# An issue order planned with measured durations, and with the price of changing between dense and small products

## The chip, the core and the metric

The kernel runs on one core of a Trainium2 chip. The metric is the device time of one execution in microseconds (us), from the first to the last instruction with what the launch adds around them. The program is built once; the order in which each engine's instructions stand is fixed then, by Python code in the kernel.

## The reference

One layer of a hybrid backbone over 512 latent tokens and 128 context tokens (together T = 640 columns), width D = 1024:

```python
mod = silu(cond) @ ada_w + ada_b                     # 48 columns of 128: shifts, scales, gates
xn = rmsnorm(x) * (1 + sc1) + sh1
rkv, glu_in, gates = split(xn @ w_in)
y_r = rwkv(shift(rkv), lora(xn), state)              # 8 heads, two directions, a scan over tokens
y_c = silu(layernorm(conv31(glu(glu_in)))) @ w_out_conv
merged = sigmoid(gate_r) * (y_r @ w_out_rwkv) + sigmoid(gate_c) * y_c
x = x + g1 * (merged @ w_o)
x = x + g2 * (relu(xn2 @ mlp_w1) ** 2 @ mlp_w2)      # D_FF = 4096
y = rmsnorm(x) * final_g
```

## The kernel before, in words

All activations lie transposed, 128 channels on the partitions and 640 token columns in two halves of 320. There are three stages.

The **setup** (up to about 60 us) forms the modulation of the first norm, xn, and the first low-rank products. The **planned stage** (about 60 to 748 us) holds everything from the input projection to the merge. The **tail** (`w_o` and the two MLP products, lines 1405 to 1562) is one unbroken run of dense products.

A **dense product** is one matmul of a 128x128 weight by 320 columns in fp32r. Each weight is split into a high and a low part (`wh`, `wl`, ScalarE and then VectorE, in `take`, line 241), so each 128x128 block costs three products (`mm3`, line 283). Twelve or 24 of them fill one PSUM bank (`ps_mm`). In the planned stage the dense jobs stand in one list, `todo` (lines 1321 to 1329): the projections of r, k, v for four head pairs p, four GLU blocks, eight gates, then two blocks of the conv side (`side_products("c")`, which need the finished conv branch), the other eight gates, then the blocks of the RWKV side `"r"` and the last of `"c"`. A job that cannot start yet is passed over. Projections and gates read xn (`xh_t`, `xl_t`); the c and r blocks read `ARGH_t`.

**Small products** are fp32 matmuls for the rest. For each head pair p: `prep` (operands), `gram` (line 765), `inverse` (mostly VectorE), `turn` and `fold`, and then the scan `chain(p)` (line 1016) of 20 steps, each of which waits for the last:

```python
mm(ps, ARGH, S)            # 4 products ps_a<-svu_w,ARGH_t
A.activation(S, ps) x2     # ScalarE empties them
mm(sp, BKt, S)             # 4 products ps_b<-svu_w,BKt_w
V.tensor_tensor(S', sp) x2 # VectorE, beside values(): 4 products and 2 ScalarE copies
```

After `chain(p)` comes `post(p)` (line 1073), the group norm of the scan's output. The conv branch is normalised in two halves by `norm_half` (line 1160). 32 columns of the modulation are formed by `ada_late` (line 621): each loads two halves of a weight column into the one buffer `adl_w` (256 KB each) and multiplies each half by four small products `ps_ad<-adl_w,csb_t`; between the halves stands `yield 2.5` (line 391), which puts the second half 2.5 us later by the planner's clock.

**What sets the order.** Each of these is a Python generator, a lane. The loop at lines 1388 to 1403 keeps an estimated time `now[0]`. At each turn it takes the most urgent lane whose due time has come (`pick`), and if there is none, one dense product (`more`). Each matmul moves the clock on by its estimated length (`mm`, line 192); instructions on VectorE, ScalarE and GpSimd get an estimated end (`Timed`, `cost_v`, `cost_a`, `cost_g`), and a lane's next due time follows from that. A lane may also be put off while `hungry()` holds (line 1372): the estimate then sees too few columns going through TensorE, by a credit that falls at `QUOTA * ENTRY / TICK` columns a microsecond. The order of TensorE, VectorE and ScalarE is issued as the loop made it (`manual_schedule`, line 1388). At run time each engine takes its own list strictly in that order and waits at an instruction whose inputs are not there.

Of the kernel before, what the change touches and what calls it, by code (L numbers as in the profile page):

```python
# [11 lines left out]
F32R = mybir.dt.float32r  # L12
# [3 lines left out]
PSUM = bass.MemoryType.PSUM  # L16

P = 128
# [35 lines left out]
NY1, NY2, NY3, CR, HG = 1, 0, 1, 1, 0  # L54
WARM, AHEAD, LATE, SKEW = 9, 3, 0, 2
NW2, GW, GM, GE = 2, 5, 3, 4
RAWS, SPLITS, SWITCH, EXTRA = ["E", "prod"], ["Gf", "Nb", "Gt"], 1, 0
NWR, NWH = 2, 3

YG, YT, YF = 4, 4, 4  # L60
LEAD, SEM, LOAD = 0.40, 0.2, 4.0
# [4 lines left out]
GAP_LORA, GAP_ADA = 1.5, 3.5  # L66
V_STEP = 20
GLU_AT = 12
TICK, ENTRY, QUOTA, CREDIT, DEBT = 3.413, 3060, 1.55, 200, 6000
CST_ID, CST_MASK, CST_SEL, CST_HSEL, CST_LATE = 0, 128, 256, 258, 260  # L70
NCST = 261

# [4 lines left out]
def hybrid_step(ctx: ExitStack, tc: tile.TileContext, I, O):  # L77
# [9 lines left out]
    now, free, last, ready = [0.0], dict(V=0.0, A=0.0, G=0.0), [0.0], {}  # L87
# [22 lines left out]
    def aps_(kw, *names):  # L110
        return sum(hasattr(kw.get(k), "shape") for k in names)

    def cost_v(name, n, src, kw):
        return 0.07 + 0.06 * aps_(kw, "scalar", "scalar1") + n / 960

    def cost_a(name, n, src, kw):
        return (0.08 if src[0].space == PSUM else 0.16) + 0.093 * aps_(kw, "scale", "bias") + n / 1400

    def cost_g(name, n, src, kw):
        return 1.9 if kw.get("op") == ALU.pow else 0.26 + n / 960  # L120
# [49 lines left out]
    warm = sut([P, 512], "warm")  # L170
# [21 lines left out]
    def mm(out, lhsT, rhs, start=True, stop=True, **kw):  # L192
        PE.matmul(out=out, lhsT=lhsT, rhs=rhs, start=start, stop=stop, **kw)  # L193
        cyc = math.prod(rhs.shape[1:]) * (1 if rhs.dtype == F32R else 2 if "is_transpose" in kw else 4)
        m = math.prod(lhsT.shape[1:])
        overlap = 128 // m if m < 128 else 128 // rhs.shape[0]
        cols = cyc * rhs.shape[0] / 128 * (1 if rhs.dtype == F32R else 0.5)
        gated["cols"] += cols
        gated["burst"] -= cols
        gated["credit"] = min(gated["credit"] + cols, CREDIT)  # L200
        kind = (m, rhs.shape[0], rhs.dtype)
        if kind != gated["kind"]:
            advance(now[0] + SWITCH * gated["drain"] / (2400 if gated["warm"] else 1200))
        gated.update(kind=kind, drain=0 if rhs.dtype == F32R else max(cyc, 256) - max(cyc / overlap, 64))
        advance(now[0] + (max(cyc / overlap, 64) + EXTRA) / (2400 if gated["warm"] else 1200))
        ready[out.name] = ("P", now[0] + SEM / 2)
        last[0] = now[0]

    def split(hi, lo, src):
# [1438 lines left out]
```

## Time and profile before

| | us |
|---|---|
| three runs | 1277.59, 1289.3, 1292.56 |
| their median | 1289.3 |
| the profiled execution | 1274.04 |
| its span, first to last instruction | 1272.3 |

The profiled execution is the shortest of the four times; 1.7 us of it lie outside the span. Times in the rows below count from the span's start. `PE` is TensorE's matmuls, `PEld` its weight loads, `DVE` VectorE, `ACT` ScalarE, `SP` the queue that issues the DMAs; `PEclk` 1.00 is 2.4 GHz and 0.50 is 1.2 GHz. An fp32 product shows as two passes, so four small products are counted as eight instructions (x8). The end of a matmul is modelled, so lengths on TensorE are best read from one start to the next.

### The profile page before, as it was taken

The page shows a single profiled execution, that of the slowest core. Times are in us where ns is not written, and L with a number is a line of the kernel's source. Part 1 is how long each engine was busy: PE and PEld are TensorE (multiplying, and loading weights), DVE is VectorE, ACT ScalarE, POOL GpSimd, SP SyncE. Part 2 cuts the span into 40 slices and gives each one's busy share as a digit, 9 for nine tenths or more (in the row PEclk, how much of TensorE's full clock was granted, in tenths as well). Part 3 has the DMA queues.
Part 4 walks back from the last instruction along what each step waited for, and adds up shares of the span by engine and source line. Part 5 has one row for each costly group of instructions (what it writes and reads, how often), then busy time and mean ns, then how long its engine had stood idle before and what let it go on. Part 6 is the DMA issues. An engine that isn't in the chain of part 4 may idle for free.

```text
span 1272.3 us, 31723 instructions
## 1 busy us (share of the span) xinstructions
PE 1219.7 (96%) x13362; PEld 1069.1 (84%) x13362; DVE 739.8 (58%) x1606; ACT 549.7 (43%) x1390; POOL 28.2 (2%) x21
## 2 busy tenths in 40 slices
PE   8998999999999999999998999999999999999996
PEld 5776786767777777777788899999999999999996
DVE  5536587757777777587444665744433443443354
ACT  5545545644565465546552233544412431342130
POOL 0100000000000000000000000000000000000000
PEclk9999998979999999999999999999999999999998
DMA  9456443222433252233216753022222222222222
GB/s 369 157 174 184 145 120 102 83 64 67 137 97 106 86 173 93 83 118 103 74 46 186 258 195 109 26 67 83 69 81 73 77 75 76 75 75 75 75 75 83
DMA packets 82574, 140.42 MB, mean 110 GB/s; under 512 B 17024, under 2 KB 31616, under 8 KB 82432
## 3 DMA queue, kind: packets, MB, share of 16 engines
q1 hardware_dynamic: 82432, 138.39, 33.7%
q8 instruction: 105, 1.72, 0.6%
q14 instruction: 37, 0.30, 0.1%
HBM read 113.52 MB, written 22.22 MB: 107 GB/s over the span
## 4 chain that ended last, share of the span: by engine, by line
PE 86%; DMA 5%; DVE 4%; issue 2%; ACT 2%; SPq 1%; POOL 0%; POOLq 0%; DVEq 0%; ACTq 0%
PE ps_mm L193 46%; PE ps_b L193 24%; PE ps_a L193 7%; PE ps_t L193 7%; PE ps_ad L193 2%; DMA adl_w<-in_adal 2%; DMA adar_s<-in_adaw 1%; DMA z<-tmp 1%; ACT tmp L106 1%; DVE Gt_w L106 0%; DMA prod_w<-in_w 0%; DVE ARGH_t L106 0%; DVE kk_t L106 0%; DVE wl_t L106 0%; DVE vS_w L106 0%
## 5 line engine op out<-in xcount | busy, mean ns | idle before, releaser
L193 PE MATMUL ps_mm<-xh_t,wh_t 128*128 128x320 f32 x648 | 217.5, 336 | 1.8 <-ACT tmp L106 1.8
L193 PE MATMUL ps_mm<-xh_t,wl_t 128*128 128x320 f32 x648 | 213.9, 330 | 0.0
L193 PE MATMUL ps_mm<-xl_t,wh_t 128*128 128x320 f32 x648 | 213.2, 329 | 0.0
L106 ACT ACTIVATE wh_t<-wr_t 128x512 fp32r<-128x512 f32 x146 | 91.7, 628 | 134.1 <-PE ps_b L193 107.0
L106 DVE TENSOR_TENSOR wl_t<-wr_t,wh_t 128x512 fp32r<-128x512 f32 x146 | 100.2, 687 | 76.0 <-ACT wh_t L106 75.2
L193 PEld LDWEIGHTS ps_mm<-xh_t,wh_t 128*128 128x128 f32 x648 | 123.6, 191 | 21.2 <-issue 11.7
L106 ACT ACTIVATE svu_w<-ps_a 64x128 f32<-64x128 f32 x320 | 86.8, 271 | 125.3 <-PE ps_a L193 119.2
L193 PEld LDWEIGHTS ps_mm<-xl_t,wh_t 128*128 128x128 f32 x648 | 123.4, 190 | 13.7 <-issue 9.0
L193 PEld LDWEIGHTS ps_mm<-xh_t,wl_t 128*128 128x128 f32 x648 | 123.5, 191 | 9.9 <-issue 4.4
L106 DVE SCALAR_TENSOR_TENSOR cacc_w<-upad_w,par_t,cacc_w 128x640 f32<-128x640 f32 x90 | 79.2, 880 | 1.9
L193 PE MATMUL ps_mm<-ARGH_t,wh_t 128*128 128x320 f32 x268 | 72.5, 312 | 0.5 <-DVE rS_w L106 0.5
L106 ACT ACTIVATE tmp<-ps_mm 128x320 f32<-128x320 f32 x80 | 34.8, 435 | 86.8 <-PE ps_mm L193 81.7
L106 DVE TENSOR_TENSOR svu_w<-ps_b,Dc_w 64x128 f32<-64x128 f32 x152 | 43.7, 287 | 48.7 <-PE ps_b L193 45.7
L193 PE MATMUL ps_mm<-ARGH_t,wl_t 128*128 128x320 f32 x204 | 64.1, 314 | 0.4 <-DVE wl_t L106 0.4
L106 ACT ACTIVATE mwh<-wr_t 128x512 fp32r<-128x512 f32 x49 | 31.0, 633 | 72.3 <-PE ps_b L193 69.4
L106 DVE SCALAR_TENSOR_TENSOR ARGH_t<-ps_mm,mod_t,ARGH_t 128x320 f32<-128x320 f32 (+2 forms) x45 | 22.6, 512 | 59.3 <-PE ps_mm L193 59.3
L106 DVE TENSOR_TENSOR tmp<-tmp 128x320 f32<-128x320 f32 x64 | 31.1, 489 | 43.3 <-ACT tmp L106 43.2
L106 DVE TENSOR_TENSOR mwl<-wr_t,mwh 128x512 fp32r<-128x512 f32 x49 | 33.8, 690 | 36.9 <-ACT mwh L106 36.9
L193 PEld LDWEIGHTS ps_mm<-ARGH_t,wh_t 128*128 128x128 f32 x268 | 48.2, 190 | 1.3 <-issue 1.0
L106 ACT ACTIVATE BKt_w<-ps_a 32x512 f32<-32x512 f32 (+3 forms) x80 | 40.0, 502 | 17.9 <-PE ps_a L193 17.0
L193 PE MATMUL ps_mm<-xl,wh_t 128*128 128x320 f32 x140 | 43.9, 314 | 0.0
L193 PE MATMUL ps_b<-ARGH_t,wl_t 128*128 128x320 f32 x140 | 43.6, 312 | 0.0
(374 smaller groups left out, 2981.6 us busy)
## 6 DMA issues: line engine op xcount, KB each, us to landing
wr_t<-in_w SPq DMA_DIRECT2D x221, 256.0 KB, 2.7
adl_w<-in_adal SPq DMA_DIRECT2D x64, 256.0 KB, 2.8
adar_s<-in_adaw SPq DMA_DIRECT2D x16, 512.0 KB, 8.4
ARGH_t<-in_x SPq DMA_DIRECT2D x8, 640.0 KB, 6.0
z<-tmp SPq DMA_DIRECT2D x32, 160.0 KB, 2.7
gate<-tmp SPq DMA_DIRECT2D x32, 160.0 KB, 1.9
tA_t<-z SPq DMA_DIRECT2D x8, 320.0 KB, 3.5
ath_t<-z SPq DMA_DIRECT2D x8, 320.0 KB, 4.4
```

The lines of the kernel that those rows point to most:

```text
L106: return f(*args, **kw)
L193: PE.matmul(out=out, lhsT=lhsT, rhs=rhs, start=start, stop=stop, **kw)
```

## The change

The planner's durations are replaced. A VectorE operation now counts 0.155 us and its elements at 960 a microsecond (480 in a scan, 550 in a transpose), where it counted 0.07, 0.06 for each operand by partition, and the elements at 960. ScalarE counts 0.16 or 0.19 at the start instead of 0.08 or 0.16, and 1180 elements a microsecond instead of 1400. A dense product counts 31 cycles more; a change from small to dense counts 250 cycles (`ENTER`) and one from dense to small 220 (`LEAVE`), beside the drain that was counted before. A product's result counts as there 0.2 us after its end (`SEM`), not 0.1. `QUOTA` falls from 1.55 to 1.25. Nothing is computed in another way, and every engine has as many compute instructions as before; only their order differs. The due times that are written as numbers (`yield 2.5`, `GAP_ADA`, `LOAD`, GpSimd's 1.9) stay.

```diff
-RAWS, SPLITS, SWITCH, EXTRA = ["E", "prod"], ["Gf", "Nb", "Gt"], 1, 0
+RAWS, SPLITS = ["E", "prod"], ["Gf", "Nb", "Gt"]
+EXTRA, ENTER, LEAVE = 31, 250, 220
-TICK, ENTRY, QUOTA, CREDIT, DEBT = 3.413, 3060, 1.55, 200, 6000
+TICK, ENTRY, QUOTA, CREDIT, DEBT = 3.413, 3060, 1.25, 200, 6000
     def cost_v(name, n, src, kw):
-        return 0.07 + 0.06 * aps_(kw, "scalar", "scalar1") + n / 960
+        return 0.155 + n / (480 if name == "tensor_tensor_scan" else 550 if name == "transpose" else 960)
     def cost_a(name, n, src, kw):
-        return (0.08 if src[0].space == PSUM else 0.16) + 0.093 * aps_(kw, "scale", "bias") + n / 1400
+        return (0.16 if src[0].space == PSUM else 0.19) + 0.093 * aps_(kw, "scale", "bias") + n / 1180
         if kind != gated["kind"]:
-            advance(now[0] + SWITCH * gated["drain"] / (2400 if gated["warm"] else 1200))
+            enters = (rhs.dtype == F32R) - (gated["kind"] is not None and gated["kind"][2] == F32R)
+            advance(now[0] + (gated["drain"] + (0, ENTER, LEAVE)[enters]) / (2400 if gated["warm"] else 1200))
-        advance(now[0] + (max(cyc / overlap, 64) + EXTRA) / (2400 if gated["warm"] else 1200))
-        ready[out.name] = ("P", now[0] + SEM / 2)
+        advance(now[0] + (max(cyc / overlap, 64) + (EXTRA if rhs.dtype == F32R else 0)) / (2400 if gated["warm"] else 1200))
+        ready[out.name] = ("P", now[0] + SEM)
```

**First place: TensorE, the scan of the last head pair (p = 3), 13 steps before its end.** `svu_w` is the scan's state S, `ps_mm` a gate, `ps_b<-ARGH_t,Gt_w` a product of `fold`, `ones_t` the sums of `norm_half`. In the kernel before, a half step there looks like this:

```order
L193 MATMUL ps_a_7883<-svu_w,ARGH_t 32x64 x4
L193 MATMUL ps_t<-ARGH_t,svu_w 64x32 x4
L193 MATMUL ps_mm<-xh_t,wh_t 128x320
L193 MATMUL ps_mm<-xl_t,wh_t 128x320
L193 MATMUL ps_mm<-xh_t,wl_t 128x320
L193 MATMUL ps_mm<-xh_t,wh_t 128x320
L193 MATMUL ps_mm<-xl_t,wh_t 128x320
L193 MATMUL ps_mm<-xh_t,wl_t 128x320
L193 MATMUL ps_mm<-xh_t,wh_t 128x320
L193 MATMUL ps_mm<-xl_t,wh_t 128x320
L193 MATMUL ps_b_7884<-svu_w,BKt_w 64x64 x4
```

In the changed kernel the last two gate products on xn stand at the top of this piece, and a whole step follows:

```order
L194 MATMUL ps_mm<-xl_t,wh_t 128x320
L194 MATMUL ps_mm<-xh_t,wl_t 128x320
L194 MATMUL ps_b_8657<-ARGH_t,Gt_w 32x32 x16
L194 MATMUL ps_a_8230<-svu_w,ARGH_t 32x64 x4
L194 MATMUL ps_t<-ARGH_t,svu_w 64x32 x4
L194 MATMUL ps_mm<-BK_w,ones_t 128x320 x2
L194 MATMUL ps_b_8231<-svu_w,BKt_w 64x64 x4
L194 MATMUL ps_a_8230<-cst_t,vS_w 32x64 x2
L194 MATMUL ps_a_8230<-cst_t,vr_w 32x64 x2
L194 MATMUL ps_mm<-BK_w,ones_t 128x320 x2
L194 MATMUL ps_a_8230<-svu_w,ARGH_t 32x64 x4
```

What moved are the dense products: when a scan begins, the dense products still to come before the first c block are 1230, 910, 594 and 310 for p = 0 to 3 in the kernel before, and 1217, 880, 432 and 80 in the changed one; 13 steps before the end of the last scan they are 234 and none.

**Second place: TensorE, between the two halves of one column of `ada_late`.** Of the 32 columns of the kernel before, the one with the fewest rows between its halves has ten:

```order
L193 MATMUL ps_ad<-adl_w,csb_t 32x128 x4
L193 MATMUL ps_mm<-xl_t,wh_t 128x320
L193 MATMUL ps_mm<-xh_t,wl_t 128x320
L193 MATMUL ps_mm<-xh_t,wh_t 128x320
L193 MATMUL ps_t<-cst_t,rh_t 64x128 x10
L193 MATMUL ps_mm<-xl_t,wh_t 128x320
L193 MATMUL ps_mm<-xh_t,wl_t 128x320
L193 MATMUL ps_mm<-xh_t,wh_t 128x320
L193 MATMUL ps_mm<-xl_t,wh_t 128x320
L193 MATMUL ps_mm<-xh_t,wl_t 128x320
L193 MATMUL ps_mm<-xh_t,wh_t 128x320
L193 MATMUL ps_ad<-adl_w,csb_t 32x128 x4
```

In the changed kernel the first column reads:

```order
L194 MATMUL ps_ad<-adl_w,csb_t 32x128 x4
L194 MATMUL ps_mm<-xh_t,wh_t 128x320
L194 MATMUL ps_mm<-xl_t,wh_t 128x320
L194 MATMUL ps_mm<-xh_t,wl_t 128x320
L194 MATMUL ps_mm<-ARGH_t 128x320
L194 MATMUL ps_t<-ARGH_t 128x320
L194 MATMUL ps_mm<-xh_t,wh_t 128x320
L194 MATMUL ps_mm<-xl_t,wh_t 128x320
L194 MATMUL ps_mm<-xh_t,wl_t 128x320
L194 MATMUL ps_ad<-adl_w,csb_t 32x128 x4
```

The same first column has 19 rows between its halves in the kernel before; over all 32 columns the middle number falls from 18 to 14. Over the whole of TensorE's order the changes between dense and small products fall from 762 to 678.

## Rows read from the trace of the kernel before

**Rows 1.** Windows by stage: length, busy us (instructions) by engine, PEclk, DMA share, GB/s

```profile
60.00:640.00 580.00, 552.67 (x8727) 427.74 (x8727) 401.62 (x903) 313.18 (x907) 15.67 (x8) 0.98 0.36 112
640.00:681.00 41.00, 38.57 (x375) 32.96 (x374) 18.63 (x51) 19.08 (x50) 3.16 (x2) 1.00 0.24 79
681.00:745.00 64.00, 58.59 (x386) 56.32 (x385) 39.27 (x77) 16.94 (x32) 0.00 (x0) 1.00 0.78 254
745.00:1272.30 527.30, 514.38 (x3504) 513.36 (x3503) 244.74 (x495) 169.05 (x330) 3.40 (x4) 0.99 0.24 76
```

**Rows 2.** Timeline of PE, start us and length: a group of small products between dense ones

```profile
243.36 0.41 PE L193 MATMUL ps_mm<-xl_t,wh_t 128*128 128x320 f32 x1
243.61 0.31 PE L193 MATMUL ps_mm<-xh_t,wl_t 128*128 128x320 f32 x1
243.75 0.31 PE L193 MATMUL ps_mm<-xh_t,wh_t 128*128 128x320 f32 x1
243.90 0.30 PE L193 MATMUL ps_mm<-xl_t,wh_t 128*128 128x320 f32 x1
244.04 0.31 PE L193 MATMUL ps_mm<-xh_t,wl_t 128*128 128x320 f32 x1
244.28 0.32 PE L193 MATMUL ps_a<-svu_w,ARGH_t 128*32 128x64 f32 x8
```

**Rows 3.** Waits of PE from 60 to 745 us: total us, times, longest

```profile
PE ps_ad L193 <- DMA adl_w<-in_adal: 8.8, 7, 2.7
PE ps_t L193 <- DVE kk_t L106: 6.5, 5, 3.1
PE ps_t L193 <- DVE vS_w L106: 5.3, 5, 1.6
```

**Rows 4.** The tile adl_w, and its products in the timeline of PE (60 and 570 us)

```profile
DMA to landing us min/median/max: 2.5/2.8/5.2
60.82 0.43 PE L193 MATMUL ps_ad<-adl_w,csb_t 128*32 128x128 f32 x8
66.41 0.43 PE L193 MATMUL ps_ad<-adl_w,csb_t 128*32 128x128 f32 x8
...
570.46 0.42 PE L193 MATMUL ps_ad<-adl_w,csb_t 128*32 128x128 f32 x8
573.65 0.43 PE L193 MATMUL ps_ad<-adl_w,csb_t 128*32 128x128 f32 x8
```

**Rows 5.** Timeline of all engines: a step of the last scan, and a dense product behind

```profile
640.20 0.32 PE L193 MATMUL ps_a<-svu_w,ARGH_t 128*32 128x64 f32 x8
640.65 0.57 ACT L106 ACTIVATE svu_w<-ps_a 64x128 f32<-64x128 f32 x2 [0.30 <-PE ps_a L193]
640.81 0.56 PE L193 MATMUL ps_mm<-xh_t,Gf_w 128*128 128x320 f32 x2
641.59 0.45 PE L193 MATMUL ps_b<-svu_w,BKt_w 128*64 128x64 f32 x8
642.09 0.61 DVE L106 TENSOR_TENSOR svu_w<-ps_b,Dc_w 64x128 f32<-64x128 f32 x2 [0.28 <-PE ps_b L193]
642.22 0.41 PE L193 MATMUL ps_mm<-xh_t,Gf_w 128*128 128x320 f32 x1
642.36 0.57 ACT L106 ACTIVATE svu_w<-ps_a 64x128 f32<-64x128 f32 x2 [0.33 <-PE ps_a L193]
```

**Rows 6.** Timeline of PE: the last scan's first and last step, post, first c block

```profile
579.15 0.32 PE L193 MATMUL ps_a<-svu_w,ARGH_t 128*32 128x64 f32 x8
656.46 0.32 PE L193 MATMUL ps_a<-svu_w,ARGH_t 128*32 128x64 f32 x8
668.02 1.09 PE L193 MATMUL ps_t<-cst_t,rh_t 128*64 128x128 f32 x16
670.33 0.41 PE L193 MATMUL ps_mm<-xh_t,wl_t 128*128 128x320 f32 x1
680.64 0.56 PE L193 MATMUL ps_mm<-ARGH_t,Nb_w 128*128 128x320 f32 x2 [1.09 <-ACT Nb_w L106]
```

**Rows 7.** The stretch at half clock and the one behind it (windows), and PE in the first

```profile
272.00:289.00 17.00, 16.80 (x180) 12.60 (x180) 7.39 (x20) 5.98 (x19) 0.00 (x0) 0.50 0.15 47
289.00:306.00 17.00, 17.00 (x226) 12.34 (x222) 13.87 (x45) 8.23 (x19) 0.00 (x0) 1.00 0.20 63
279.08 0.44 PE L193 MATMUL ps_a<-svu_w,ARGH_t 128*32 128x64 f32 x8
281.91 0.70 PE L193 MATMUL ps_b<-svu_w,BKt_w 128*64 128x64 f32 x8
282.53 0.32 PE L193 MATMUL ps_a<-cst_t,vS_w 64*32 64x64 f32 x2
```

## Prediction

> **What bounds the kernel now.** I read the windows by stage first. In the planned stage (60 to 640 us) PE is busy 552.7 of 580 us, in the tail 514.4 of 527.3, and no other engine comes near [rows 1]. So time goes down only if PE needs less for its products, or waits less. The room is small: the idle time of PE between 60 and 640 us is 27.3 us, and between 640 and 681 us 2.4 us [rows 1]. The list of PE's waits says what ends that idle time: 8.8 us are the loads of `adl_w`, and 6.5 and 5.3 us are VectorE's emptying of the one bank `ps_t` inside a group norm, which stands in one piece of code and cannot be filled by any order [rows 3].
>
> "Perfetto Trace Analysis" of the Trainium skill, section "Identifying the Most-Contended Engine", says that matmul busy time is a bad measure of the distance from the limit and that the share of weight loads is a good one. By it PE has 580 - 427.7 = 152 us of room in the planned stage [rows 1], and a better order could win far more than I allow. I follow the idle time instead: small products hold PE while their weight loads are short, and in the tail, where nothing but dense products stands, both readings come to the same (514.4 and 513.4).
>
> The second thing to read is where the dense products stand, because they are what fills PE while a scan step waits. In the trace the last scan begins at 579.15 and its last step stands at 656.46; the post work ends at 670.33, and the first c block starts at 680.64 [rows 6]. In the order of before, dense products lie in every half step up to that point. In the changed order the scan of p = 3 starts with 80 of them left instead of 310, and for its last 13 steps, for `post(3)` and up to the first c block there are none. The c blocks cannot come forward: they need the conv branch.
>
> **The change part by part.**
>
> First, fewer changes between dense and small. From one dense product to the next it is 0.14 to 0.15 us (243.61 to 243.75); from the first one behind a small group 0.25 (243.36 to 243.61), from the last one in front of a group 0.24 (244.04 to 244.28) [rows 2]. A visit to the small products thus costs 0.10 + 0.09 = 0.19 us. Over the whole order there are 762 - 678 = 84 changes fewer; in the planned stage alone 88, which is 44 visits: 44 x 0.19 = 8.4 us less. The last product of a group also runs longer, but groups of unlike small products now follow each other 32 times more; these two take most of each other back, and I leave them out. Bounds: 0 to -12.
>
> Second, the loads of `adl_w`. There is one buffer, so the second half's load starts when the first half's products are done, and lands 2.5 to 5.2 us after its issue, 2.8 in the middle. The shortest distance between two halves is 570.46 to 573.65, 3.2 us; the first one took 60.82 to 66.41, 5.6 us [rows 4]. Half a column is 0.36 us of products, so about 3.0 us of other work are needed between them, more in the first 120 us where the weights' loads share the queue. The due time of 2.5 us is unchanged, but the planner's clock was slow: it charged a dense product 320/2400 = 0.133 us, where a row shows 0.146, and nothing for the 0.19 of a visit. With the new numbers 2.5 planned us are close to 2.5 real ones. Counting the products between the halves in the changed order with the lengths of rows 2 and 5, 17 of 32 columns have less than 3.0 us between them, where before it was two. Ten of these miss by about 0.5 us; seven early ones by some 1.5. That is 15 us, against the 8.8 of before, which go: +7. What waits behind it on PE is everything, since PE takes its list in order. Bounds: 0 (loads land at their minimum) to +20 (all 17 as late as the first one, 2 us and more).
>
> Third, the bare end of the last scan. What was hidden there is now in the open. One step is: four products to the end of ScalarE's two copies, 640.20 to 641.22, 1.02 us; then four products to the end of the copies behind `values`, 641.59 to 642.93, 1.34 us [rows 5]. With 0.1 us for each of the two releases of PE (an estimate; ScalarE starts 0.13 us behind the products in rows 5) a step cannot take less than 2.4 to 2.6 us. PE itself works only 0.61 + 0.63 = 1.24 us in it (640.20 to 640.81, 641.59 to 642.22). An idle PE has lost its clock in this trace: at 1.2 GHz the same groups take 0.44, 0.70 and 0.32 us instead of 0.32, 0.45 and 0.25 [rows 5, 7], some 0.4 us a step. So a step takes about 2.9 us: 13 x 2.9 = 38. The conv branch's normalisation runs on the same ScalarE and VectorE in this time; I add 3 us for that. From the last step to the first c block it took 24.2 us (656.46 to 680.64 [rows 6]), of which 111 gate products (counted in the order) of 0.147 us are 16 us. Without them 8 us of PE's work remain, but the group norm is a chain through ScalarE, VectorE and GpSimd, and the c weights must be split: between 8 and 24 I take 16, the middle. Together 38 + 3 + 16 = 57 us. PE's own work in it is 13 x 1.24 = 16 for the steps and about 12 for the rest (two sums of `norm_half` and `post`, the first group of which is the 1.09 us of rows 6), 28 us, which the kernel before did too. About 3 us of waits stood in this stretch before and are replaced (the 2.4 us of idle time in 640 to 681 [rows 1]). Loss: 57 - 28 - 3 = +26. Bounds: 13 steps of 2.4 and 8 us behind them, 39 us, +8; 13 steps of 4.1 us, which is what a step took with its dense products (77.3 us from the first to the last, 19 steps [rows 6]), and 24 behind them, 77 us, +46.
>
> On the clock, "TensorE: Matmul & The Clock Gate" of the Trainium skill, section "Terms", puts the price of a throttled time at that time x (1 - K/N). If the whole bare stretch of 57 us went at 1.2 GHz, this would be 28 us on top. The rows give less: at half clock 180 instructions went through in 17 us, in the next 17 us 226 [rows 7], a fifth fewer and not half, since small products wait on their neighbours more than on the array. I keep the rows' 0.4 us a step, 5 us in all.
>
> Nothing is expected behind that point: the c and r blocks stand in the same number and nearly the same sequence (first c block to the end of the span 591.7 us [rows 1, 6]), and the tail is the same list.
>
> Sum: -8 + 7 + 26 = +25. The profiled execution took 1274.0 us (span 1272.3), so 1299 on its basis. It is the fastest of four; the middle of 1274.0, 1277.6, 1289.3 and 1292.6 is 1283.4, and the median of the three runs 1289.3. A measured median should stand as far above the fastest as it did before: I add 9.4 us for that and forecast 1308. Each change below is likewise set on 1283.4.
>
> **Rivals.**
>
> The waits of before go, and the bare stretch is cheap (not slower). The estimate now has the measured lengths, so a lane should be taken when its operands are really there. For it: 27.3 us of idle PE in the planned stage, of which 27.3 - 6.5 - 5.3 = 15.5 can be moved by an order, and two stretches where the clock fell. Against it: the longest of these waits hangs on a due time that did not change, and three quarters of the last scan's dense cover (310 to 80) is gone in the order itself. With all 15.5 gone, -8 for the changes and the bare stretch at its lower bound of +8, the sum is -15, about 1268; with the bare stretch at +20 it is -3, 1280. It decides when the bare stretch costs less than the 24 us that the other two give.
>
> The bare stretch is dearer (much slower). ScalarE has in it four scan copies of 0.28 us and up to two more small ones a step, and 17 operations for each half of the conv norm; every engine takes its list in order, so a norm copy that waits for GpSimd holds up a scan copy behind it. Steps of 3.7 us, between my 2.9 and the 4.1 of before, and 24 us behind them give 72 - 28 - 3 = +41; with -8 and +15 for the loads this is +48, 1331.
>
> The order change comes to nothing (same): the earlier dense work is not lost, and the scan was not late. For it: all 310 products are done in any case. Against it: they lie ahead of the scan and not beside it. Here PE would reach the last scan 15 us sooner than the count of its products says; +0 to +8, 1283 to 1291.
>
> **How the numbers follow.** A measurement of this kernel can tell about 1% (13 us) from no change. Forecast, +13 to +38: 0.60. Waits gone: 0.12, half of it beyond -1%. Dearer: 0.16. Nothing: 0.12. Faster by over 1%: 0.06. Within 1%: 0.06 + 0.12 = 0.18. Slower: 0.60 + 0.16 = 0.76. The range leaves out half of the first rival and the upper end of the second: 1281 to 1335.
>
> **What would show it.** Right: between about 645 and 700 us PE is busy for half the time or less with nothing dense in it; its clock falls there; the waits of PE on `svu_w` rise from almost nothing to 10 us or more; the first c block starts at 700 to 712 instead of 680.6, and from there to the end it is 590 to 595 us as before. The waits for `adl_w` rise from 8.8 to about 15. From a dense product to the next it stays 0.146. Wrong: the first c block starts before 690, which would mean that steps of the scan are shorter than 2.4 us or that PE came to the last scan earlier than its count of products says; or the loss lies in the c and r blocks, behind that point.

## The result: slower by 3.8%, twice the loss that was forecast

| | before | after |
|---|---|---|
| median of four runs, us | 1286.2 (1277.6 to 1292.6) | 1337.1 (1326.4 to 1337.8) |
| ratio of after to before, 95% interval | | 1.038 (1.030 to 1.047) |
| profiled execution, us | 1274.0 | 1326.4 |
| its span, us | 1272.3 | 1324.6 |

The forecast was +25 us (1308, range 1281 to 1335); measured are +51. The direction and the main term were right, the size was not, and the time lies 2 us outside the range. Both profiled executions lie 11 to 12 us below the medians, and as far apart (52 us) as these are (51).

**The windows by stage** of the changed kernel, against [rows 1], with the same columns (length, then busy us and instructions of PE, PEld, DVE, ACT, POOL, then PEclk, DMA share, GB/s). The first three stretches have the same limits as in [rows 1]:

```profile
60.00:640.00 580.00, 536.42 (x8151) 423.63 (x8150) 379.42 (x844) 288.55 (x813) 15.31 (x7) 0.96 0.36 113
640.00:681.00 41.00, 40.72 (x625) 31.97 (x623) 21.79 (x48) 21.81 (x80) 0.85 (x1) 0.91 0.09 28
681.00:745.00 64.00, 47.15 (x424) 38.53 (x424) 27.11 (x73) 24.70 (x70) 3.22 (x2) 0.58 0.24 72
745.00:1324.60 579.60, 560.64 (x3799) 557.89 (x3797) 277.75 (x560) 183.07 (x358) 3.40 (x4) 0.99 0.28 92
```

PE's idle time up to 640 us is 43.6 us where it was 27.3, and between 681 and 745 us 16.9 where it was 5.4, with a granted clock of 0.58.

**The waits of PE** from 60 to 745 us, against [rows 3]:

```profile
PE ps_ad L194 <- DMA adl_w<-in_adal: 21.8, 19, 3.2
PE ps_t L194 <- ACT Gf_w L107: 6.3, 1, 6.3
PE ps_mm L194 <- DVE wl_t L107: 5.0, 1, 5.0
PE ps_a L194 <- ACT svu_w L107: 4.8, 7, 0.7
PE ps_t L194 <- DVE vS_w L107: 4.6, 5, 1.4
PE ps_t L194 <- DVE kk_t L107: 3.9, 6, 0.9
```

The loads of `adl_w` cost 21.8 us where they cost 8.8. The next two, one wait each, are as good as new (`wl_t` cost 0.4 us before, `Gf_w` nothing), and neither was in the forecast.

**The last scan in PE's timeline**, against [rows 5, 6]: its first step, the last gate product on xn, the first step behind it, its last step, `post(3)`, the first c block:

```profile
635.71 0.32 PE L194 MATMUL ps_a<-svu_w,ARGH_t 128*32 128x64 f32 x8
...
663.11 0.31 PE L194 MATMUL ps_mm<-xh_t,wl_t 128*128 128x320 f32 x1
...
663.73 0.32 PE L194 MATMUL ps_a<-svu_w,ARGH_t 128*32 128x64 f32 x8
...
707.84 0.44 PE L194 MATMUL ps_a<-svu_w,ARGH_t 128*32 128x64 f32 x8 [0.69 <-ACT svu_w L107]
719.91 1.97 PE L194 MATMUL ps_t<-cst_t,rh_t 128*64 128x128 f32 x16 [2.54 <-POOL rh_t L107]
723.44 0.90 PE L194 MATMUL ps_mm<-ARGH_t,wh_t 128*128 128x320 f32 x2
```

From the last gate product to the first c block it is 60.3 us: 44.1 us of bare steps (a bare step has no dense product in it; 663.73 to 707.84) and 15.6 us behind them. One step and the start of the next (timeline of PE, ScalarE, VectorE) show what a step waits for: PE waits for ScalarE's copies, and operations of the conv norm stand between these in ScalarE's list. In the first step one of them (`pt_t<-BK_w`) fits into a gap and holds nothing up. In the second, `BK_w` runs until 699.47 and the scan's copy starts at 699.49, though its products started at 698.47; the first step takes 2.9 us, the second 3.4.

```profile
694.94 0.57 ACT L107 ACTIVATE svu_w<-ps_a 64x128 f32<-64x128 f32 x2 [0.27 <-PE ps_a L194]
695.41 0.55 ACT L107 ACTIVATE pt_t<-BK_w,hlnb_t 128x320 f32<-128x320 f32 x1
695.56 0.44 PE L194 MATMUL ps_a<-svu_w,ARGH_t 128*32 128x64 f32 x8 [0.69 <-ACT svu_w L107]
696.12 0.57 ACT L107 ACTIVATE svu_w<-ps_a 64x128 f32<-64x128 f32 x2 [0.17 <-PE ps_a L194]
696.45 0.98 PE L194 MATMUL ps_b<-svu_w,BKt_w 128*64 128x64 f32 x8
697.47 0.61 DVE L107 TENSOR_TENSOR svu_w<-ps_b,Dc_w 64x128 f32<-64x128 f32 x2 [0.16 <-PE ps_b L194]
697.87 0.55 ACT L107 ACTIVATE svu_w<-ps_a 64x128 f32<-64x128 f32 x2 [0.72 <-PE ps_a L194]
698.47 0.44 PE L194 MATMUL ps_a<-svu_w,ARGH_t 128*32 128x64 f32 x8 [0.67 <-ACT svu_w L107]
698.91 0.56 ACT L107 ACTIVATE BK_w<-BK_w,par_t 128x320 f32<-128x320 f32 x1
699.49 0.57 ACT L107 ACTIVATE svu_w<-ps_a 64x128 f32<-64x128 f32 x2
```

**Where the 52 us are.** Both kernels issue the same products, so the two lists can be laid side by side by position. For each kind of neighbours on PE (dense to dense, dense to small, and so on) I took the mean distance from start to start in the trace of before, without the places where PE stood idle, and added these up along each list: this is the list's own work. What a trace takes above it is waiting and slow clock.

| part of PE's list | before | after | difference |
|---|---|---|---|
| own work up to the first c block | 630 | 620 | -10 |
| above it, up to the last gate product of after (about the 5400th product) | 48 | 71 | +23 |
| above it, from there to the first c block | 2 | 32 | +30 |
| above it, in the two c blocks (96 products; 16.7 us before, 26.4 after) | 3 | 12 | +10 |
| above it, behind them | 8 | 7 | -1 |

The sum is +52, the difference of the spans. The split depends on how the neighbours are sorted: by shape, by tile or only as dense and small, with or without the idle places, the first row comes out between -8 and -16, the second between +18 and +25, the third between +30 and +35, and the c blocks at +10.

### The profile page after: what moved, and what is told of

It is laid out like the page before. It is cut to its first block, busy times and chain, and to the rows that moved or that the text cites. A ratio compares the mean times of both kernels' runs of the same rounds, so it can differ in the third digit from the quotient of the medians.

```text
span 1324.6 us, 31765 instructions
## 1 busy us (share of the span) xinstructions
PE 1240.0 (94%) x13362; PEld 1090.7 (82%) x13362; DVE 741.3 (56%) x1606; ACT 549.1 (41%) x1390; POOL 28.8 (2%) x21
## 4 chain that ended last, share of the span: by engine, by line
PE 82%; DMA 6%; DVE 6%; ACT 3%; issue 2%; POOL 0%; SPq 0%; POOLq 0%; DVEq 0%; ACTq 0%
PE ps_mm L194 43%; PE ps_b L194 24%; PE ps_t L194 7%; PE ps_a L194 7%; DMA adl_w<-in_adal 4%; PE ps_ad L194 2%; DMA pg_t<-g 1%; ACT svu_w L107 1%; DVE vS_w L107 1%; DVE prod_w L107 1%; DVE Gt_w L107 1%; DVE cacc_w L107 1%; DVE ARGH_t L107 0%; DMA ARGH_t<-in_x 0%; DVE wl_t L107 0%
## 5 line engine op out<-in xcount | busy, mean ns | idle before, releaser
L194 PE MATMUL ps_mm<-xh_t,wh_t 128*128 128x320 f32 x680 | 226.3, 333 | 0.4 <-ACT tmp L107 0.3
L194 PE MATMUL ps_mm<-xh_t,wl_t 128*128 128x320 f32 x680 | 225.3, 331 | 0.0
L194 PE MATMUL ps_mm<-xl_t,wh_t 128*128 128x320 f32 x680 | 225.2, 331 | 0.0
L194 PEld LDWEIGHTS ps_mm<-xl_t,wh_t 128*128 128x128 f32 x680 | 131.4, 193 | 13.9 <-issue 8.6
L194 PEld LDWEIGHTS ps_mm<-xh_t,wl_t 128*128 128x128 f32 x680 | 131.1, 193 | 14.0 <-issue 9.8
L194 PEld LDWEIGHTS ps_mm<-xh_t,wh_t 128*128 128x128 f32 x680 | 131.2, 193 | 13.2 <-issue 6.4
L107 ACT ACTIVATE svu_w<-ps_a 64x128 f32<-64x128 f32 x320 | 86.8, 271 | 122.5 <-PE ps_a L194 117.8
L194 PE MATMUL ps_mm<-ARGH_t,wh_t 128*128 128x320 f32 x284 | 77.5, 318 | 1.1 <-ACT wh_t L107 0.6
L194 PEld LDWEIGHTS ps_mm<-ARGH_t,wh_t 128*128 128x128 f32 x284 | 52.3, 196 | 2.0 <-ACT wh_t L107 0.9
L194 PE MATMUL ps_ad<-adl_w,csb_t 128*32 128x128 f32 x512 | 28.4, 295 | 22.0 <-DMA adl_w<-in_adal 21.8
L194 PEld LDWEIGHTS ps_mm<-ARGH_t,wl_t 128*128 128x128 f32 x212 | 40.8, 192 | 5.4 <-DVE wl_t L107 5.4
```

The costliest lines, as they stand in the source:

```text
L107: return f(*args, **kw)
```

## The experiments

A time from one run is held against the profiled execution of the changed kernel, 1326.4. The four runs of that kernel span 11 us, so a difference of less than that says nothing by its time; there the parts of the trace have to speak.

**1. The old lengths of VectorE and ScalarE, everything else new.**

```diff
     def cost_v(name, n, src, kw):
-        return 0.155 + n / (480 if name == "tensor_tensor_scan" else 550 if name == "transpose" else 960)
+        return 0.07 + 0.06 * aps_(kw, "scalar", "scalar1") + n / 960
     def cost_a(name, n, src, kw):
-        return (0.16 if src[0].space == PSUM else 0.19) + 0.093 * aps_(kw, "scale", "bias") + n / 1180
+        return (0.08 if src[0].space == PSUM else 0.16) + 0.093 * aps_(kw, "scale", "bias") + n / 1400
```

> The changed kernel with the old lengths for VectorE and ScalarE; the new ones for TensorE, SEM and QUOTA 1.25 stay. In its order no step of the last scan is bare (570 dense products left when it starts, instead of 80) and there are 692 changes instead of 678. My theory (the bare end of the scan cost about 30 us, the c blocks right behind it 10, the loads of adl_w 13, and the lengths of VectorE and ScalarE are what made the scan late): the bare end and the loss in the c blocks go, the waits on adl_w are about 12 to 16 us instead of 21.8, and the time is 1275 to 1295, level with the kernel before. Rival (the loss is spread over the whole planned stage by the new lengths for TensorE and the lower QUOTA): it stays above 1310.

Measured: 1284.0 us (ratio to before 0.998, 0.994 to 1.001). The profiled execution took 1291.1 us and has 15.9 us of waits on `adl_w`. Its windows from 640 us on, in the columns above:

```profile
640.00:681.00 41.00, 39.28 (x269) 38.37 (x266) 18.43 (x31) 18.79 (x38) 0.00 (x0) 0.99 0.48 153
681.00:745.00 64.00, 62.12 (x415) 60.54 (x414) 28.93 (x55) 16.59 (x32) 0.00 (x0) 1.00 0.62 190
```

1.9 us of idle PE stand between 681 and 745 us instead of 16.9, at full clock: the bare end and the loss in the c blocks went together. The rival falls. Which of the two engines' lengths does it in the changed kernel, this run does not tell; experiment 10 takes ScalarE's alone, on the kernel before. That longer lengths push a lane's small products back, and so let dense ones go first, follows from the planner's code and from the counts in the orders; no run shows it step by step.

**2. QUOTA alone.**

```diff
-TICK, ENTRY, QUOTA, CREDIT, DEBT = 3.413, 3060, 1.55, 200, 6000
+TICK, ENTRY, QUOTA, CREDIT, DEBT = 3.413, 3060, 1.25, 200, 6000
```

> The kernel before with QUOTA 1.25 instead of 1.55 and nothing else. Its order has 648 changes instead of 762 (57 visits fewer) and no bare step; when the last scan starts, 506 dense products are left instead of 310. My theory (a visit costs 0.19 us, and QUOTA is not what made the scan late): 57 x 0.19 = 11 us less on TensorE, a few us of it given back in waits on adl_w (nine columns with little between their halves instead of six), so 0.5% faster, 1273 to 1288. Rival (QUOTA alone does the damage): 1310 or more.

Measured: 1293.3 us (ratio 1.006, 1.002 to 1.011). Neither theory. PE's waits from 640 to 745 us show why:

```profile
PE ps_mm L193 <- ACT wh_t L106: 13.3, 2, 12.7
PE ps_t L193 <- ACT pt_t L106: 3.6, 1, 3.6
PE ps_t L193 <- ACT u_t L106: 1.7, 1, 1.7
```

The scan has its cover, but the norm of the conv branch stands last in this order, with 7 dense products behind its sums (216 before). They run out at 670 us, and PE has next to nothing until the first c block at 696.5: about 26 us. I had looked for bare steps of the scan only. Up to the last gate product the kernel was indeed ahead; the end took it all back.

**3. No load for the second half of a modulation column** (the weights of the first half are multiplied again, so half of each column is left out).

```diff
-            raw = wt([P, KD // 2, P], "adl")
-            DMA.dma_start(out=raw, in_=I["adal"][col - 16, :, 4 * j:4 * j + 4, :])
+            if j == 0:
+                raw = wt([P, KD // 2, P], "adl")
+                DMA.dma_start(out=raw, in_=I["adal"][col - 16, :, 0:4, :])
```

> The changed kernel without the second half's load of adl_w: the second half of each of the 32 columns multiplies the weights of the first half again (the second half of each column is left out of the computation). TensorE's order stays. My theory: the waits on adl_w fall from 21.8 us to 5 or less, TensorE reaches the last gate product 15 to 20 us earlier, and the bare end stays at about 60 us; 1310 to 1322 in all. Rival (another wait takes the place of the load, since lanes that were covered by it come up next): the time falls by less than 8 us.

Measured (one run): 1308.2 us, 18 less. The waits on `adl_w` fell to 2.0 us, the last gate product came at 645 instead of 663, and the stretch behind it took 60.8 us, as in the changed kernel (60.3). Nearly all that the loads cost is real; the wait of 6.3 us on `Gf_w` stayed (6.5).

**4 and 5. Dense products that nobody needs in the bare end: clock or latency?** The first kernel asked for the bank anew for each product:

```diff
+        if steps[3] and 3 not in chained and not any(j[1] is gate for j in todo):
+            mm(bank("ad")[:, 0:H2], xh[:, 0, 0:P], xh[:, 0, 0:H2])
+            return True
```

> The changed kernel with 172 dense products more, which multiply xn by itself into a bank that nobody reads, in the bare end of the last scan and only there; nothing is left out. They let TensorE's list there look as in the kernel before. Theory (the bare end is a chain of latencies; the clock of 1.2 GHz that was granted there is a smaller part): the granted clock goes up to 2.4 GHz, the stretch from the last gate product to the first c block stays at 52 to 60 us, and the c blocks behind it, which began at 1.2 GHz, take 2 to 4 us less. Rival (the clock sets the pace of the bare steps): with the clock at 2.4 GHz the stretch falls to 45 us or less although TensorE has 25 us more work in it.

Measured (one run): 1443.9 us. It answers nothing: there is one buffer for this bank (`ps_ad`), so each added product's weight load waited 0.41 us for the product before, and they stood 0.69 us from start to start where dense ones stand 0.15. The second kernel keeps the bank and allows six products a step (the expectation calls the first ones fp32; the trace has them in one pass each, as dense ones):

```diff
+        if steps[3] and 3 not in chained and not any(j[1] is gate for j in todo) and fillt.count(steps[3]) < 6:
+            if not fillt:
+                fillt.append(bank("ad"))
+            mm(fillt[0][:, 0:H2], xh[:, 0, 0:P], xh[:, 0, 0:H2])
+            fillt.append(steps[3])
+            return True
```

> The changed kernel with 82 dense products more (xn by itself, into a bank that nobody reads), at most six in a step of the last scan where nothing else is left; the first such kernel was made with 172 fp32 products of 0.62 us at 1.2 GHz, so it told nothing of the clock. These add 12 us of TensorE's work at 2.4 GHz to a stretch in which it was busy for about 40 of 60 us. Theory (a chain of latencies): whether or not the clock rises, the stretch from the last gate product to the first c block stays between 52 and 64 us. Rival (the clock sets the pace): if the clock is 2.4 GHz there, the steps take 2.6 us or less and the stretch 50 us or less in spite of the added work.

Measured (one run): 1338.9 us; the stretch took 65.2 us, 1 more than my theory's upper end. Windows of it (columns as above), and the starts of three steps in PE's timeline:

```profile
707.00:724.00 17.00, 14.59 (x191) 11.28 (x183) 8.82 (x30) 10.25 (x30) 0.00 (x0) 0.85 0.12 32
724.00:735.00 11.00, 8.46 (x97) 6.08 (x92) 4.55 (x16) 4.47 (x14) 0.00 (x0) 1.00 0.04 13
```

```profile
718.71 0.32 PE L194 MATMUL ps_a<-svu_w,ARGH_t 128*32 128x64 f32 x8
...
722.30 0.32 PE L194 MATMUL ps_a<-svu_w,ARGH_t 128*32 128x64 f32 x8
...
725.07 0.32 PE L194 MATMUL ps_a<-svu_w,ARGH_t 128*32 128x64 f32 x8
```

Its last five steps ran at 2.4 GHz (0.32 us for a group that takes 0.44 at 1.2) and still took 2.8 to 3.6 us, against 2.9 to 3.4 at half clock in the changed kernel. The rival wanted 2.6 us or less. But the clock rose for only a part of the stretch, and the six added products of a step take about 0.9 us (estimate: six times 0.147), so the run bounds the clock's part and doesn't measure it. Experiment 7 does.

**6. A longer due time between the halves, on top of experiment 1.**

```diff
-            yield 2.5 if k0 == 0 else 0.0
+            yield 3.6 if k0 == 0 else 0.0
```

> The changed kernel with the old lengths for VectorE and ScalarE, and with the due time between the two halves of a modulation column at 3.6 instead of 2.5 us. In its order one of 32 columns has too little between its halves (ten without the longer due time), no step of the last scan is bare, 565 dense products are left when it starts, and there are 658 changes. My theory (15.9 us of waits on adl_w stood in the kernel without the longer due time, and what waits is the load's own 2.8 us): they fall to 5 us or less, and the time is 8 to 14 us less than that kernel's 1284, about 1270 to 1276, 1% faster than the kernel before. Rival (the modulation columns come later and something else runs out): 1280 to 1295.

Measured: 1270.3 us (ratio 0.989, 0.985 to 0.993), 1.1% faster than the kernel before, at the lower end of what I expected. The first of PE's waits from 60 to 745 us, and the windows behind 640 us:

```profile
PE ps_ad L194 <- DMA adl_w<-in_adal: 6.5, 4, 3.1
```

```profile
640.00:681.00 41.00, 41.00 (x281) 41.00 (x280) 11.95 (x18) 13.08 (x25) 0.00 (x0) 1.00 0.50 159
681.00:745.00 64.00, 61.36 (x409) 59.61 (x408) 35.83 (x71) 15.79 (x31) 0.00 (x0) 1.00 0.70 229
```

The loads cost 6.5 us instead of 15.9, and PE is idle for 2.6 us from 640 to 745 us, all of it at full clock.

**7. The same due time on the changed kernel alone.** The edit is that of experiment 6.

> The changed kernel with 3.6 us between the halves of a modulation column and nothing else. In its order two columns are short instead of 23, but three dense products are left when the last scan starts, and 19 of its steps are bare instead of 13. My theory (both are terms of one sum): the waits on adl_w fall from 21.8 to 6 us or less, -16; six bare steps more at 3.0 us less 1.24 of their own work, +10; 1325 to 1335, about level with the changed kernel. Rival (the waits on adl_w were the larger part): 1315 or less.

Measured (one run): 1308.8 us. The rival's number. The waits on `adl_w` fell to 1.7 us and the one on `Gf_w` to 0.5, and at the last gate product PE stood 42 us above its own work instead of 71: 29 us, not 16, of which these two waits are 26. The bare end grew more than I thought: 86.8 us, of which 40.8 are own work, so 46 instead of 32, or 2.3 us for each of six more steps where I had 1.8.

This run also measures the clock's part of a bare step. One step ran at 2.4 GHz, the last of several at 1.2 GHz, with the same 32 instructions on PE and nothing added (PE's timeline, from one step's start to the next):

```profile
645.08 0.32 PE L194 MATMUL ps_a<-svu_w,ARGH_t 128*32 128x64 f32 x8
...
647.77 0.32 PE L194 MATMUL ps_a<-svu_w,ARGH_t 128*32 128x64 f32 x8 [0.69 <-ACT svu_w L107]
...
685.44 0.44 PE L194 MATMUL ps_a<-svu_w,ARGH_t 128*32 128x64 f32 x8 [0.69 <-ACT svu_w L107]
...
688.50 0.44 PE L194 MATMUL ps_a<-svu_w,ARGH_t 128*32 128x64 f32 x8 [0.69 <-ACT svu_w L107]
```

It took 2.7 us; the seven such steps at half clock took 2.9 to 3.4, 3.2 in the mean (3.1 in the changed kernel). Experiment 10 has one more bare step at 2.4 GHz, without any hold on ScalarE, of 2.4 us (672.61 to 675.05), where the shortest ones at half clock took 2.9. So the clock is worth about 0.5 us of a bare step, and most of the step's length stays without it. These are two steps, and the norm's operations fall differently in each, so the figure is good to some 0.2 us.

**8. QUOTA 1.25 with the conv lane more urgent** (to mend experiment 2).

```diff
-URGENT = dict(scan=0, split=0.3, shift=1.45, post=1, side=0.9, solve=1, prep=1.5, lora=2, ada=4, out=4.5, branch=0.5, conv=1.6)
+URGENT = dict(scan=0, split=0.3, shift=1.45, post=1, side=0.9, solve=1, prep=1.5, lora=2, ada=4, out=4.5, branch=0.5, conv=1.2)
```

> The kernel before with QUOTA 1.25 and with the conv lane's urgency at 1.2 instead of 1.6, and nothing else. With QUOTA 1.25 alone the norm of the conv branch came last: 7 dense products were left behind its sums, TensorE then stood 26 us nearly idle, and the whole was 0.6% slower than before. Here 285 are left behind these sums and 425 when the last scan starts; the changes fall to 568. My theory (visits cost 0.19 us, and what was lost with QUOTA alone was only that the dense products ran out ahead of the norm): the 26 us go, some 5 us more of adl_w waits come (18 columns short instead of nine), and the time is 1268 to 1278, 1% faster than before. Rival (fewer changes mean a lower clock or longer waits elsewhere, which was what made QUOTA 1.25 slow): 1284 or more.

Measured: 1332.1 us (ratio 1.039, 1.033 to 1.046). A clear miss. The bare 26 us did go, and its list has the least own work of all these kernels that keep a cover (609 us to the first c block, 21 less than before). But PE stood 131 us above that work at the first c block, against 50. Its window up to 640 us and PE's two longest waits from 60 to 745 us:

```profile
60.00:640.00 580.00, 520.80 (x8143) 410.47 (x8142) 377.65 (x845) 284.29 (x812) 15.06 (x7) 0.88 0.34 104
```

```profile
PE ps_ad L193 <- DMA adl_w<-in_adal: 21.4, 13, 4.9
PE ps_a L193 <- ACT svu_w L106: 9.3, 15, 0.7
```

With 568 changes the dense products stand in longer runs and the small ones in longer runs between them. There the steps wait for their copies, the loads for their landing, and the clock falls (0.88). How much of the loss comes from the longer runs, and how much from the conv lane's new place, these two runs don't separate: experiment 2 has 648 changes and lost 0.6%. The theory that fewer changes are worth their visits falls, as a forecast of the whole; the price of a visit is not touched.

**9. Only the due time of post(3)'s last product.**

```diff
-        yield 3.0
+        yield 3.0 if p < 3 else 6.0
         V.tensor_tensor(out=y, in0=y, in1=g, op=ALU.mult)
```

> The changed kernel with one due time changed: in post(3) the product with g stands 6.0 planned us behind the load of g instead of 3.0, so that VectorE's splits of the c weights stand ahead of it in VectorE's list. My theory (VectorE waited 3 us for the load of g, and the splits and TensorE's c products behind it): the wait of 5.0 us in the c blocks goes, and they take 20 to 23 us instead of 26.4. Rival (the splits are late for another reason, their load or ScalarE's copy): a wait of 4 us or more stays at the same product.

Measured (one run): 1324.5 us, too near to tell from 1326.4, and the c blocks take 25.3 us instead of 26.4. In the changed kernel VectorE's list had the product with g ahead of the splits, and PE's c block waited behind both (timeline of VectorE and PE):

```profile
727.88 0.83 DVE L107 TENSOR_TENSOR vS_w<-vS_w,pg_t 128x640 f32<-128x640 f32 x1 [3.05 <-DMA pg_t<-g]
728.62 1.29 DVE L107 TENSOR_TENSOR wl_t<-wr_t,wh_t 128x512 fp32r<-128x512 f32 x2
...
729.36 0.64 PE L194 MATMUL ps_mm<-ARGH_t,wl_t 128*128 128x320 f32 x1 [5.02 <-DVE wl_t L107]
```

With the edit that wait is 1.1 us, and the next one takes most of its place, 6.6 instead of 3.9: ScalarE's `Nb_w` stands behind its copies of post(3)'s output, which is now stored later. PE's timeline with the edit:

```profile
721.96 0.64 PE L194 MATMUL ps_mm<-ARGH_t,wl_t 128*128 128x320 f32 x1 [1.14 <-DVE wl_t L107]
745.19 6.92 PE L194 MATMUL ps_mm<-ARGH_t,Nb_w 128*128 128x320 f32 x24 [6.57 <-ACT Nb_w L107]
```

The mechanism (a wait at the head of an engine's list) is right, the price of mending one place is not: the whole chain behind the last scan is late.

**10. The new lengths of ScalarE alone, on the kernel before.**

```diff
     def cost_a(name, n, src, kw):
-        return (0.08 if src[0].space == PSUM else 0.16) + 0.093 * aps_(kw, "scale", "bias") + n / 1400
+        return (0.16 if src[0].space == PSUM else 0.19) + 0.093 * aps_(kw, "scale", "bias") + n / 1180
```

> The kernel before with the two new constants of ScalarE's lengths and nothing else. Its order has none of the dense products left when the last scan starts (310 before), so all 20 steps of it are bare, and 678 changes. My theory (the cover of the last scan decides, whatever the new length was that took it away): 20 steps of 3 us and 16 us behind them stand where TensorE has 20 x 1.24 + 12 = 37 us of its own work, +39; the c blocks behind them cost 10 more as in the changed kernel: 1286 + 49, between 1315 and 1345. Rival (it takes the new lengths of all engines together): 1280 to 1300.

Measured: 1337.1 us (ratio 1.040, 1.035 to 1.044). The time is as expected; two constants of an engine that is busy for half the time are as bad as the whole change. The parts are not as expected. From the last gate product (601.6) to the first c block (732.6) it is 131 us, where the theory had 76 for the steps and what follows them. The 39 us before the scan's first step (640.8) are bare as well, and PE is busy for half of them (window, columns as above):

```profile
600.00:641.00 41.00, 21.34 (x646) 18.44 (x644) 32.66 (x74) 11.99 (x29) 1.96 (x1) 0.57 0.19 61
```

Ahead of that PE loses less than in the kernel before: when both have done 565 us of their own work, 26 us stand above it instead of 45, and this makes up for it. So the time was met by luck in part; that a lost cover is dear stands. The c blocks behind the bare end take 27.3 us.

**11. The new lengths of TensorE alone, QUOTA left at 1.55.**

```diff
-RAWS, SPLITS, SWITCH, EXTRA = ["E", "prod"], ["Gf", "Nb", "Gt"], 1, 0
+RAWS, SPLITS = ["E", "prod"], ["Gf", "Nb", "Gt"]
+EXTRA, ENTER, LEAVE = 31, 250, 220
...
-        ready[out.name] = ("P", now[0] + SEM / 2)
+        ready[out.name] = ("P", now[0] + SEM)
```

> The kernel before with the new lengths for TensorE alone (EXTRA, ENTER, LEAVE, SEM) and QUOTA left at 1.55. The order puts nearly all dense products first: 864, 168, 0 and 0 are left at the four scans, 40 steps are bare, 112 changes stand where there were 762. My theory (a charge for dense products and QUOTA are one setting: at 1.55 the planner is always short of columns): the 325 visits fewer give 60 us, and 40 bare steps with 3.0 - 1.24 each cost 70, with the bare prep and post between them 50 to 90 more; 1340 to 1400. Rival (the changes were the cost): 1230 or less.

Measured (one run): 1430.5 us, worse than my range. The list's own work fell by some 60 us as counted, and some 250 us of waits and slow clock stand above it at the first c block. The charges of TensorE and QUOTA are one setting: with the same charges and QUOTA 1.25 (experiment 1) the time is 1284.0.

**12. Experiment 6 with QUOTA 1.4.**

```diff
-TICK, ENTRY, QUOTA, CREDIT, DEBT = 3.413, 3060, 1.25, 200, 6000
+TICK, ENTRY, QUOTA, CREDIT, DEBT = 3.413, 3060, 1.4, 200, 6000
```

> The changed kernel with the old lengths for VectorE and ScalarE, 3.6 us between the halves of a modulation column, and QUOTA 1.4 instead of 1.25 (the best kernel so far has 1.25). 448 dense products are left at the last scan instead of 565, two columns are short instead of one, 678 changes instead of 658. My theory (QUOTA sets how evenly the dense products are spread, and with them the granted clock; the kernel with 1.25 spent 51 us of its first 1000 at 1.2 GHz, the kernel before 31): some 20 us less at 1.2 GHz, each worth 0.2, is 4 us, less 2 us for 10 visits more: 1264 to 1272. Rival (the cover is thinner and the time is the same or worse): 1272 or more.

Measured: 1269.2 us (ratio 0.987, 0.983 to 0.991). The time is within the range, and the interval overlaps that of experiment 6, so the two are not told apart. The reason doesn't hold: its profile has 61 us at 1.2 GHz in the first 1000, more and not less than the 51 of experiment 6; its waits on `adl_w` are 0.8 us. This and experiment 6 are the versions that beat both kernels, the one before by little over 1%.

## Why the prediction was right in direction and half in size

**First term, fewer changes, -8.** The list's own work is 10 us less. Right as a term. Experiment 8 shows that it can't be sold alone: what shortens the list takes the cover from the waits.

**Second term, the loads, +7: the step that failed most.** It counted 17 columns with less than 3.0 us of other work between their halves and let ten miss by 0.5 us and seven by 1.5, some 15 us. In the trace 17 columns do wait between their halves, and 15 of them have 1.2 to 3.0 us of other work there (two have 3.2 and 3.3), so the count was good. The need of 3.0 us was too small: in these 17 columns it is 2.65 to 5.2 us from the end of the first half to the start of the second, 3.7 in the middle, since the load has to be issued first and then lands in 2.5 to 4.7 us. Their waits are 1.13 us in the mean, 19.2 us. Two more waits, 2.6 us, stand ahead of a column's first half, where the term did not look. Together that is 21.8 us, +13 where +7 stood. The trace of before could have said that the line is not sharp: four of its seven waits are in columns with 3.5 to 4.1 us of other work, 0.4 to 2.2 us each.

And the term had nothing else in it: the part of the list up to the last gate product lost 23 us. The other 10 are the wait on `Gf_w`, 6.3, and an estimated 3 to 4 of slow clock (up to that product 44 us at 1.2 GHz instead of 27; the 17 us more at the fifth that [rows 7] show). The wait on `Gf_w` is the same mechanism as in the c blocks, on ScalarE (timeline of the changed kernel, VectorE, ScalarE and PE):

```profile
488.02 0.82 DVE L107 TENSOR_TENSOR vS_w<-vS_w,pg_t 128x640 f32<-128x640 f32 x1 [2.20 <-DMA pg_t<-g]
...
491.39 0.53 ACT L107 ACTIVATE vS_w<-ps_mm,m_t 128x320 f32<-128x320 f32 x1 [7.04 <-DMA out<-vS_w]
...
493.98 0.40 ACT L107 ACTIVATE Gf_w<-ps_t,cst_t 128x160 f32<-128x160 f32 x1
...
494.43 0.78 PE L194 MATMUL ps_t<-Gf_w,prod_w 32*32 32x16 f32 x43 [6.35 <-ACT Gf_w L107]
```

A load of g holds VectorE, its product is stored, the store holds the buffer `vS_w`, ScalarE waits for that buffer for 7 us, and a small copy that PE needs stands five places behind it. I had read the order on PE alone, and this wait can only be seen with the lists of four engines side by side. Experiments 3 and 7 bear the term out from both sides: without the second loads 18 us go, with the longer due time 29 (the order moves as well there).

**Third term, the bare end, +26.** 60 us measured for 57, and +30. The two parts come out as said: 44 us of steps for 41, 15.6 behind them for 16. The first of them is partly luck: these 44 us hold 12 step lengths of 3.7 us, not 13 of 2.9. Three steps with the norm's sums take 3.8, 4.5 and 7.4 us, for which the 3 us set aside were too few; the others take 2.9 to 3.8. The granted clock was 1.2 GHz for 61 us from 673.5, that is from 10 us into the bare end until 11 us into the c blocks. "TensorE: Matmul & The Clock Gate" of the Trainium skill, section "Terms", would have put 28 us on top of the 57; the stretch came out 3 above them. Here the trace differs from the rule: of a step of about 3 us at half clock the clock is worth about 0.5 (experiment 7), near the 0.4 that the prediction took from [rows 5, 7], and not half. Experiment 1 undoes the term, and experiment 10 brings a bare end back by another cause.

Of the signs that the prediction named, the fall of the clock and the dearer loads came. Others did not: the first c block started at 723.4 and not by 712, PE's waits on `svu_w` rose from 1.5 to 4.8 us and not to 10, and PE counts as busy for four fifths of the bare end (window below) and not for half of it or less. At half clock the same small groups fill more of a step.

```profile
663.00:724.00 61.00, 48.89 (x550) 37.04 (x550) 25.34 (x78) 35.11 (x109) 4.07 (x3) 0.59 0.05 15
```

**"Nothing is expected behind that point": wrong by 10 us.** The prediction had named a loss there as a sign that it is wrong. The two lists there are nearly the same, but their operands are not equally ready. When the scan ends under its cover, `post(3)`, its store and the copies behind it are done or begun beside dense work. In the kernel before, VectorE's product with g, which waits for its load in both kernels, stands 4 us ahead of the first c block (680.64):

```profile
676.56 0.83 DVE L106 TENSOR_TENSOR vS_w<-vS_w,pg_t 128x640 f32<-128x640 f32 x1 [3.36 <-DMA pg_t<-g]
```

In the changed kernel it stands 4 us behind it (727.88, first c block 723.44; experiment 9). When the scan ends bare, all this is still to come when the first c block starts. PE's waits in the c blocks are 8.9 us (5.0 on `wl_t`, 3.9 on `Nb_w`), about 7 more than before, and the low clock adds some 2.3 (estimate: 19 dense products there stand 0.267 us apart instead of 0.147). Wherever the scan ends bare, the c blocks take 25 to 32 us (the changed kernel, experiments 7, 9, 10, 11) instead of 14 to 17 (before, experiments 2 and 12).

**The rivals.** "The waits of before go" fell: PE's idle time up to 640 us grew from 27.3 to 43.6. "The bare stretch is dearer" came nearest in time (1331), but not by its mechanism: its step of 3.7 us is the mean of the trace, with the three steps that hold the norm's sums, yet the stretch took 60 us and not the 72 it gives. The rest of the loss lies ahead of the stretch and behind it. "The order change comes to nothing" fell; in experiments 1 and 10 the loss goes and comes with the count of dense products left at the last scan.

The step that failed, then, is the sum's boundary, and in it the need of 3.0 us for a load. I priced the waits that the trace of before had, and the one stretch that PE's order showed, and took the rest of the list as it was. Of the 27 us that the sum lacks on the profiled executions (52 for 25), 16 lie in the second term, 10 in the c blocks, for which it had nothing, and 4 in the bare end; the first term and the part behind the c blocks give 3 back.

## What to carry to other kernels

Here exact lengths in the planner were worth nothing by themselves: its rates, due times and quotas had been set against the old ones (experiments 6, 7 and 11), and what counted was which work was left to cover the last chain of waits. Before such a change is timed, count in the order how much free work is left when each serial chain starts and when each late operand's work begins, on all engines. And where an order turns a stretch bare, price what starts behind it too, because everything that the cover hid is late at once.

## What was not expected of the hardware

PE can count as busy while its clock stays low: in the first kernel of experiments 4 and 5 it was busy for 37.4 of 40 us, by the profile's modelled ends, with the added products waiting on each other, and the granted clock was 0.50 (1.2 GHz) throughout, in the window

```profile
720.00:760.00 40.00, 37.38 (x105) 20.57 (x105) 2.71 (x7) 7.53 (x21) 0.85 (x1) 0.50 0.00 0
```

And a serial step of four small products, two copies, four products and two copies is only a little shorter at 2.4 GHz than at 1.2: 2.4 and 2.7 us against 2.9 to 3.4 (experiment 7), though the products alone took 0.32 instead of 0.44 us for a group. Where dense products follow each other, at the start of the c blocks, the same fall costs nearly half the pace: 0.267 us apart instead of 0.147.
